# A diffusion backbone's first projection: products from raw streams, feature tile by feature tile, and modulation products 512 columns wide

## Chip, core and metric

One NeuronCore of a Trainium2 chip runs the whole program. The metric is the device time of one execution in microseconds (us), lower is better.

## What is computed

Two layers over 512 latent tokens and 256 context tokens of 1024 features. Layer 0 mixes tokens by latent attention (MLA), layer 1 by a gated linear recurrence (HGRN2); each is followed by a SwiGLU FFN. Every sub-layer takes a normalized input that is scaled and shifted by values ("modulation") made from a vector c, one set for latent and one for context tokens. The part around the change, cut from the reference:

```python
def rms_norm(x, w):
    y = x * lax.rsqrt(jnp.mean(x * x, axis=-1, keepdims=True) + EPS)
    return y * w

mod_l = jnp.split(jax.nn.silu(c) @ ada_w[i] + ada_b[i], 6, axis=-1)        # shift, scale, gate, shift, scale, gate
mod_c = jnp.split(jax.nn.silu(c_ctx) @ ada_w[i] + ada_b[i], 6, axis=-1)
a_l = rms_norm(x, norm1_w[i]) * (1 + mod_l[1]) + mod_l[0]
a_c = rms_norm(h_ctx, norm1_w[i]) * (1 + mod_c[1]) + mod_c[0]
...
# MLA, for latent and context tokens alike
cq, ckv, kr = jnp.split(a @ w_in, [384, 384 + 256], axis=-1)               # w_in: 1024 x 704
q = split_heads(rms_norm(cq, q_norm_w) @ w_uq, 8)
kv = split_heads(rms_norm(ckv, kv_norm_w) @ w_ukv, 8)
k_rope = rms_norm(kr, kr_w)
```

## The kernel before

Features lie on the 128 partitions: a stream is 8 feature tiles (`KD`) by 768 tokens (`NT`), in 6 token tiles, 0 to 3 latent and 4, 5 context. Products run in fp32r with operands split in a high and a low half: high by high, high by low and low by high, three matmuls for one product (`mm3m`, L101 to L110; `mm3`, L92 to L99).

**Modulation** (`ada`, L150 to L168). 96 units of 128 columns, 48 for each layer; layer 0's units 0 to 7 are the first sub-layer's shift, 8 to 15 its scale. A call makes n units (always 4). Each unit loads one tile of 512 KB, [128, 8 feature tiles x 128 columns], into one of four slots of the ring `wf`, and runs 8 f32 matmuls with a stationary operand of 32 columns, feature tile k into partitions 32 (k mod 4) on, that is, into one of four column groups of the array; the profile shows each as two passes (L158). ScalarE copies the rows out of PSUM, TensorE transposes them, VectorE adds the four groups and the bias.

**The input projection** (`mla_in`, L324 to L424). SP's queue issues all loads in the order of the program: first x (16 loads), then modulation units 0 to 3 and 8 to 11, WIN for features 0 to 3, units 4 to 7 and 12 to 15, WIN 4 to 7, the tables BC and ROPE. ScalarE squares x and VectorE adds up (L187 to L194); a transpose, a reduction, a power on GpSimd and an f32 matmul against ones spread each token's factor over all partitions (`norm_rb`, L197 to L217). Then, in two halves of four feature tiles, `norm` (L219 to L232) writes the normalized, scaled and shifted activations in two halves, a_hi and a_lo, and the WIN weights are split, high by ScalarE (L359), low by GpSimd (L360). `proj` (L383 to L396) multiplies: per token tile 8 feature tiles, 384 and 320 columns, three matmuls each; tiles 0 and 1 together, then 2, 3, 4, 5. For each token tile follow squares on ScalarE (L407), the three root factors (`rsqrt`), the normalized c (L412, L413), the rotary part on GpSimd, six transposes into the one PSUM buffer `tp2` (L419), and the copies into cn_hi, kr_hh (L420, L421) and cn_lo, kr_lo (L422, L423).

**Attention** (`mla_attend`) starts from cn_hi and cn_lo. The WUP weights are loaded into `wf`, cast by ScalarE (L83) and split by GpSimd (L84). For every head and group of three token tiles come products, squares (L470), factors, rotary steps on GpSimd, transposes (L489), then scores (L514 to L518). In heads 1 to 7 `ada` calls for later sub-layers stand behind the head at a lowered priority (`ADA_HEAD`, `ada_m`).

**Order.** The Tile framework plans the order on each engine from its own costs: of what is ready by them it takes what stands first in the program, moved by the priorities in `PRIO`. PSUM has eight banks: `sc` and `tp2` of two banks each, `ov`, two `L`, one `M`.

## Time and profile before

| | us |
|---|---|
| median of 3 runs | 1847.92 |
| lowest and highest run | 1844.15, 1857.01 |
| the profiled execution | 1853.65 |
| its span, first to last instruction | 1851.9 |

A profile shows one execution of the program. "Busy" is the time in which an engine works on an instruction; a matmul's end is modelled, so starts tell more than ends. A row of the timeline gives start, duration, engine, line, operation, out<-in by the program's names and, in brackets, the engine's idle time before it and what ended that. PE is TensorE, DVE VectorE, ACT ScalarE, POOL GpSimd, SP the queue that issues DMAs.

### The profile page before, as it was taken

Reading aid. Unit: us, or ns where it says so; the run is one execution under the profiler, and the core shown is the slowest. Engines: PE = TensorE matmul, PEld = TensorE weight load, DVE = VectorE, ACT = ScalarE, POOL = GpSimd, SP = SyncE. Lnnn points to the kernel's source line nnn. Section 1 sums busy time; section 2 is a strip of 40 time slices with the busy share of each in tenths; the row PEclk is TensorE's granted clock in tenths of the full one; section 3 lists DMA queues with packets and bytes.
Section 4 is the critical chain, followed back from the end, with each engine's and each line's share of the span. In section 5 each row is a group of like instructions: output and inputs, shape, how many; then the busy total and the mean of one; then the engine's idle time right before and its main releaser. Section 6 shows DMA issues by size and latency. Waiting matters only on the chain. (4 is left out here: it accounts for less than half of the span.)

```text
span 1851.9 us, 33106 instructions
## 1 busy us (share of the span) xinstructions
PE 1755.5 (95%) x13708; PEld 1591.8 (86%) x13708; DVE 1016.3 (55%) x1646; ACT 762.6 (41%) x1467; POOL 760.6 (41%) x528
## 2 busy tenths in 40 slices
PE   4889999999899999999999999999998889999999
PEld 3878989788799999988887888888896779999888
DVE  5567887741754445432203666575745278888400
ACT  4355565532554344432213332423333255555411
POOL 2333342216566666643344554554643440000442
PEclk9999999999999999999999999999999989999999
DMA  7412032523222322254224121111115233333331
GB/s 268 137 39 73 25 116 98 170 74 122 103 86 97 104 96 103 81 168 136 86 71 148 60 69 47 61 55 58 58 35 191 94 137 103 103 115 103 108 118 49
DMA packets 55015, 183.61 MB, mean 99 GB/s; under 512 B 6224, under 2 KB 8528, under 8 KB 54864
## 3 DMA queue, kind: packets, MB, share of 16 engines
q1 hardware_dynamic: 53424, 173.62, 28.5%
q10 hardware_dynamic: 1440, 7.86, 1.2%
q8 instruction: 108, 1.77, 0.4%
q14 instruction: 43, 0.35, 0.1%
HBM read 171.50 MB, written 9.96 MB: 98 GB/s over the span
## 5 line engine op out<-in xcount | busy, mean ns | idle before, releaser
L84 POOL TENSOR_TENSOR wl<-wf,wh 128x1024 fp32r<-128x1024 f32 (+2 forms) x130 | 287.0, 2214 | 438.9 <-ACT wh L83 436.5
L83 ACT CAST wh<-wf 128x1024 fp32r<-128x1024 f32 (+2 forms) x130 | 122.9, 947 | 226.2 <-PE L L98 102.5
L97 PE MATMUL q<-op,sh 128*128 128x384 f32 (+1 forms) x640 | 197.3, 310 | 1.0 <-ACT sh L622 1.0
L98 PE MATMUL q<-op,sh 128*128 128x384 f32 (+1 forms) x640 | 197.6, 310 | 0.0
L99 PE MATMUL q<-op,sl 128*128 128x384 f32 (+1 forms) x640 | 194.9, 310 | 0.0
L97 PEld LDWEIGHTS q<-op,sh 128*128 128x128 f32 x640 | 120.3, 188 | 1.5 <-ACT sh L622 1.5
L98 PEld LDWEIGHTS q<-op,sh 128*128 128x128 f32 x640 | 120.3, 188 | 0.0
L99 PEld LDWEIGHTS q<-op,sl 128*128 128x128 f32 x640 | 119.5, 188 | 0.0
L623 POOL TENSOR_TENSOR sl<-wf,sh 128x1024 fp32r<-128x1024 f32 (+1 forms) x40 | 88.7, 2218 | 56.4 <-ACT sh L622 56.4
L98 PE MATMUL L<-op,sh 128*128 128x256 f32 (+1 forms) x360 | 110.4, 307 | 0.0
L99 PE MATMUL L<-op,sl 128*128 128x256 f32 (+1 forms) x360 | 110.3, 306 | 0.0
L97 PE MATMUL L<-op,sh 128*128 128x256 f32 (+1 forms) x360 | 110.3, 306 | 0.0
L1060 DVE TENSOR_TENSOR X<-X,T 128x512 f32<-128x512 f32 x96 | 78.1, 855 | 47.0 <-PE lv L985 45.9
L557 DVE SCALAR_TENSOR_TENSOR xl<-L,mod,xl 128x512 f32<-128x512 f32 x24 | 17.9, 750 | 153.8 <-PE L L99 149.8
L622 ACT CAST sh<-wf 128x1024 fp32r<-128x1024 f32 x80 | 66.7, 834 | 70.2 <-PE L L98 32.7
L98 PE MATMUL L<-f_lo,wh 128*128 128x512 f32 (+1 forms) x240 | 89.1, 371 | 0.0
L97 PE MATMUL L<-f_hi,wh 128*128 128x512 f32 (+1 forms) x240 | 89.0, 371 | 0.0
L99 PE MATMUL L<-f_hi,wl 128*128 128x512 f32 (+1 forms) x240 | 88.5, 369 | 0.0
L158 PE MATMUL L<-adaw,s 128*32 128x128 f32 x1216 | 57.1, 297 | 29.5 <-DMA adaw<-in_ADA 29.3
L975 POOL TENSOR_SCALAR km<-X 128x512 f32<-128x512 f32 x40 | 29.4, 737 | 125.5 <-DVE X L1060 76.4
L622 ACT CAST sh<-sb 128x1024 fp32r<-128x1024 f32 x40 | 42.0, 1050 | 88.5 <-PE q L98 46.6
L158 PEld LDWEIGHTS L<-adaw,s 128*32 128x32 f32 x1216 | 34.8, 116 | 46.1 <-DMA adaw<-in_ADA 17.2
(466 smaller groups left out, 5585.3 us busy)
## 6 DMA issues: line engine op xcount, KB each, us to landing
wf<-in_W SPq DMA_DIRECT2D x104, 512.0 KB, 3.5
adaw<-in_ADA SPq DMA_DIRECT2D x96, 512.0 KB, 4.4
wf<-in_HW SPq DMA_DIRECT2D x32, 512.0 KB, 3.5
wf<-in_W SPq DMA_DIRECT2D x24, 384.0 KB, 3.2
gd<-s SPq DMA_DIRECT2D x10, 768.0 KB, 3.5
g<-gd ACTq DMA_DIRECT2D x10, 768.0 KB, 4.7
wf<-in_W SPq DMA_DIRECT2D x16, 320.0 KB, 3.0
wf<-in_MWO SPq DMA_DIRECT2D x8, 512.0 KB, 4.1
```

Of the source, the lines that this page charges most:

```text
L83: nc.scalar.copy(hi[:, :n], w[:, :n])
L84: nc.gpsimd.tensor_sub(lo[:, :n], w[:, :n], hi[:, :n].bitcast(F32))
L97: nc.tensor.matmul(out, lhsT=lh, rhs=rh, start=(new and i == 0), stop=False, skip_group_check=more)
L98: nc.tensor.matmul(out, lhsT=lh, rhs=rl, start=False, stop=False, skip_group_check=more)
L99: nc.tensor.matmul(out, lhsT=ll, rhs=rh, start=False, stop=(i == n - 1), skip_group_check=more)
L158: nc.tensor.matmul(rows_ps[32 * j:32 * j + 32, i * P:(i + 1) * P], lhsT=self.s32[:, k, :], rhs=w[:, k * P:(k + 1) * P], start=(k < 4), sto ...
L557: nc.vector.scalar_tensor_tensor(xk, po, gate[:, s:s + 1], xk, op0=ALU.mult, op1=ALU.add)
L622: nc.scalar.copy(hi[:, :n], s)
L623: (nc.vector if j in on_dve else nc.gpsimd).tensor_sub(lo[:, :n], s, hi[:, :n].bitcast(F32))
L975: nc.gpsimd.tensor_scalar(km.rearrange("p (m b r) -> p m b r", b=2, r=L), mix, 1.0, 0.0, op0=ALU.mult, op1=ALU.add)
L1060: nc.vector.tensor_tensor(v, v, t, op=ALU.mult)
```

## The change

- **Raw products.** `mla_in` splits x itself into x_hi and x_lo and scales the WIN weights instead: `scaled(k, s)` makes high and low halves of WIN's feature tile k times norm weight times (1 + scale), for latent (s = 0) or context tokens (s = 1), the high half on ScalarE, the low on VectorE. The factor of each token and the shift come in afterwards, in `norms`: product times the token's factor, plus the row shift @ WIN.
- **Loop over feature tiles.** Loads of x, scale units, WIN and shift units are interleaved by pairs of features. Each feature tile is multiplied at once for tiles 0 to 3 (512 and 192 columns) and for 512 columns of tile 4; the rest of tile 4 and tile 5 follow behind the loop (`left`), with the weights scaled anew. All raw weights are kept, in the memory where cn_hi and cn_lo come to lie.
- **Shift rows** (`shift_rows`), inside the loop between feature tiles 6 and 7: f32 products of the shifts with the raw weights, through column groups and a summing matrix, all through the one bank `M`.
- **Norms by pairs** of token tiles, out of an SBUF copy; **turn** does the transposes and copies for all six tiles behind the loop and `left`. The first WUP weights are fetched ahead of `turn`.
- **Wide modulation.** `ada` loads the same bytes cut the other way: a load holds RING / (128 n) feature tiles by all n units' columns. With n = 4 that is two feature tiles by 512 columns, with n = 2 (the new calls in `mla_in`) four by 256; a call of four units has 8 matmuls of 512 columns instead of 32 of 128.

```diff
+NIN = QR + KVR + DR
+WUP_CUT = ((0, 768), (768, 1664))
...
-PRIO = {"hg_head": 1000, "ada_m": -500, "ada_n": -300}
+PRIO = {"shw": 600, "hg_head": 1000, "ada_m": -500, "ada_n": -300}
...
     def ada(self, l, u0, n, pool, bank):
         nc = self.nc
         rows_ps = bank()
-        for i in range(n):
+        g, c0 = divmod(u0, 4)
+        src = self.a["ADA"][l, g].rearrange("p (k c) -> p k c", k=KD)[:, :, c0 * P:(c0 + n) * P]
+        kn = RING // (n * P)
+        for k0 in range(0, KD, kn):
             w = self.ring.tile([P, RING], F32, tag="wf", name="adaw", bufs=4)
-            nc.sync.dma_start(out=w[:, :D], in_=self.a["ADA"][l, u0 + i])
-            for k in range(KD):
+            nc.sync.dma_start(out=w.rearrange("p (k c) -> p k c", k=kn), in_=src[:, k0:k0 + kn])
+            for k in range(k0, k0 + kn):
                 j = k % 4
-                nc.tensor.matmul(rows_ps[32 * j:32 * j + 32, i * P:(i + 1) * P], lhsT=self.s32[:, k, :],
-                                 rhs=w[:, k * P:(k + 1) * P], start=(k < 4), stop=(k >= 4))
+                nc.tensor.matmul(rows_ps[32 * j:32 * j + 32, :n * P], lhsT=self.s32[:, k, :],
+                                 rhs=w[:, (k - k0) * n * P:(k - k0 + 1) * n * P], start=(k < 4), stop=(k >= 4))
...
-    def mla_in(self, es, mla, a_hi, a_lo):
+    def mla_in(self, es, mla, x_hi, x_lo):
...
-        w_hi = st.tile([P, KD, 704], F32R, name="w_hi")
-        w_lo = st.tile([P, KD, 704], F32R, name="w_lo")
+        wp = self.pool(es, "wp", side="right")
+        shw = wp.tile([P, 2, NIN], F32, name="shw")
+        rms = wp.tile([P, 2, TT], F32, name="rms")
...
-        with ExitStack() as es1:
-            ap = self.pool(es1, "adap")
-            x = [ap.tile([P, KD, c1 - c0], F32, name=f"x0{s}") for s, c0, c1 in SEGS]
-            for k in range(KD):
...
-                    self.sq_add(ap, acc, x[s][:, k, :], s, k, c0, c1, nc.vector, 2)
-            rb = ps.tile([P, NT], F32, tag="tp2", name="rb")
...
-                    self.ada(0, k0, 4, ap, self.M)
-                    self.ada(0, KD + k0, 4, ap, lambda: ps.tile([P, 512], F32, tag="ov", name="ov"))
-                self.norm_scale(0, 0, ks)
-                self.norm(0, 0, x, rbs, SEGS, ap, a_hi, a_lo, ks)
-                for k in ks:
-                    w = self.ring.tile([P, RING], F32, tag="wf", name="wf", bufs=4)
-                    last = nc.sync.dma_start(out=w[:, :704], in_=a["WIN"][:, k, :])
-                    nc.scalar.copy(w_hi[:, k, :], w[:, :704])
-                    nc.gpsimd.tensor_sub(w_lo[:, k, :], w[:, :704], w_hi[:, k, :].bitcast(F32))
-
-        with self.tc.issue_after(last.ins):
-            nc.sync.dma_start(out=bc, in_=a["BC"].partition_broadcast(P))
-            nc.sync.dma_start(out=rt, in_=a["ROPE"])
-        self.cn = cn = self.pool(mla, "cn")
...
+        wide, even = ((0, 512), (512, NIN)), ((0, QR), (QR, NIN))
+        def scaled(k, s):
+            sc = self.nsc[(0, 0)][:, k, s:s + 1]
+            hi, lo = (wp.tile([P, NIN], F32R, tag=n, name=f"w_{n}", bufs=3) for n in ("hi", "lo"))
+            nc.scalar.activation(hi, raw[k], AF.Identity, scale=sc)
+            nc.vector.scalar_tensor_tensor(lo, raw[k], sc, hi.bitcast(F32), op0=ALU.mult, op1=ALU.subtract)
+            return hi, lo
+        def products(outs, k, w):
+            hi, lo = w
+            for o, t, (c0, c1), new, end in outs:
+                c = slice(t * P, (t + 1) * P)
+                mm = nc.tensor.matmul
+                mm(o, lhsT=x_hi[:, k, c], rhs=hi[:, c0:c1], start=(k == 0 and new), stop=False)
+                mm(o, lhsT=x_hi[:, k, c], rhs=lo[:, c0:c1], start=False, stop=False)
+                mm(o, lhsT=x_lo[:, k, c], rhs=hi[:, c0:c1], start=False, stop=(k == KD - 1 and end))
+        def norms(t0, sums):
+            p2 = wp.tile([P, 2, NIN], F32, tag="pre", name="pre", bufs=2)
+            for o, t, (c0, c1), _, _ in sums:
+                if t0 <= t < t0 + 2:
+                    nc.vector.scalar_tensor_tensor(p2[:, t - t0, c0:c1], o, rms[:, 1, t:t + 1], shw[:, t0 // 4, c0:c1], op0=ALU.mult, op1=ALU.add)
...
+            r = tmp.tile([P, 2, 3], F32, tag="r", name="r")
+            self.rsqrt(r.rearrange("p a b -> p (a b)"), ss.rearrange("p a b -> p (a b)"), tmp, "in")
+            c = tmp.tile([P, 2, 6, P], F32, tag="c", name="c", bufs=2)
+            m = tmp.tile([P, 2, DR], F32, tag="m", name="m")
+            nc.vector.tensor_tensor(m, p2[:, :, 640:NIN], r[:, :, 2:3].broadcast_to([P, 2, DR]), op=ALU.mult)
+            self.rope(c[:, :, 5, :], m, ktab[:, t0:t0 + 2], tmp)
+            for i in range(2):
+                cf = c[:, i].rearrange("p a b -> p (a b)")
+                for j, w0 in ((0, BC_Q), (1, BC_KV)):
+                    c0, c1 = cuts[j]
+                    nc.vector.scalar_tensor_tensor(cf[:, c0:c1], p2[:, i, c0:c1], r[:, i, j:j + 1], bc[:, w0:w0 + c1 - c0], op0=ALU.mult, op1=ALU.mult)
+            return c
+        def turn(t0, c):
+            for i in range(2):
+                ts = slice((t0 + i) * P, (t0 + i + 1) * P)
+                tp = ps.tile([P, 6, P], F32, tag="tp2", name="tp")
+                for j in range(6):
+                    nc.tensor.transpose(tp[:, j, :], c[:, i, j, :], self.ident)
+                nc.scalar.copy(cn_hi[:, :, ts], tp[:, 0:5, :])
+                nc.scalar.copy(kr_hh[:, ts], tp[:, 5, :])
+                nc.vector.tensor_sub(cn_lo[:, :, ts], tp[:, 0:5, :], cn_hi[:, :, ts].bitcast(F32))
+                nc.vector.tensor_sub(kr_lo[:, ts], tp[:, 5, :], kr_hh[:, ts].bitcast(F32))
...
+        self.cn = cn = self.pool(mla, "cn")
+        raw = [cn.tile([P, 4, NIN], F32, tag=t, name="raw") for t in ("cn_hi", "cn_lo")]
+        raw = [raw[k // 4][:, k % 4] for k in range(KD)]
...
+        with ExitStack() as es1:
+            ap = self.pool(es1, "adap")
+            acc = ap.tile([P, NT], F32, name="acc")
...
+            big = [ps.tile([P, 1024], F32, tag=tag, name="pp") for tag in ("sc", "tp2")]
+            rest = [self.L() for _ in range(2)]
+            ov = ps.tile([P, 512], F32, tag="ov", name="ov")
+            lat = [(big[t // 2][:, 512 * (t % 2):512 * (t % 2) + 512], t, wide[0], True, True) for t in range(4)]
+            lat += [(rest[t // 2][:, 192 * (t % 2):192 * (t % 2) + 192], t, wide[1], t % 2 == 0, t % 2 == 1) for t in range(4)]
+            lat = [lat[i] for t in range(4) for i in (t, 4 + t)]
+            for k0 in range(0, KD, 2):
+                ks = range(k0, k0 + 2)
+                for k in ks:
+                    xk = self.ring.tile([P, NT], F32, tag=("wh", "wl")[k % 2], name="xk", bufs=3)
+                    nc.sync.dma_start(out=xk, in_=a["XT"][:, k, :])
+                    nc.scalar.copy(x_hi[:, k, :], xk)
+                    nc.vector.tensor_sub(x_lo[:, k, :], xk, x_hi[:, k, :].bitcast(F32))
+                    if k == 0:
+                        nc.scalar.activation(acc, xk, AF.Square)
+                        continue
+                    sq = ap.tile([P, NT], F32, tag="sq", name="sq", bufs=2)
+                    nc.scalar.activation(sq, xk, AF.Square)
+                    if k == KD - 1:
+                        nc.vector.scalar_tensor_tensor(acc, acc, EPS * KD, sq, op0=ALU.add, op1=ALU.add)
+                    else:
+                        nc.vector.tensor_add(acc, acc, sq)
+                self.ada(0, KD + k0, 2, ap, self.M)
+                self.norm_scale(0, 0, ks)
+                for k in ks:
+                    if k < KD - 1:
+                        nc.sync.dma_start(out=raw[k], in_=a["WIN"][:, k, :])
+                    if k == KD - 2:
+                        for c0, c1 in ((0, 4), (4, TT)):
+                            tp = self.M()
+                            for t in range(c0, c1):
+                                nc.tensor.transpose(tp[:, (t - c0) * P:(t - c0 + 1) * P], acc[:, t * P:(t + 1) * P], self.ident)
+                            nc.vector.tensor_reduce(rms[:, 0, c0:c1], tp[:, :(c1 - c0) * P].rearrange("p (t f) -> p t f", f=P), axis=AX.X, op=ALU.add)
+                        nc.gpsimd.tensor_tensor(rms[:, 1, :], rms[:, 0, :], self.half.broadcast_to([P, TT]), op=ALU.pow)
+                        nc.vector.tensor_scalar(rms[:, 1, :], rms[:, 1, :], math.sqrt(D), None, op0=ALU.mult)
+                    products(lat, k, scaled(k, 0))
+                    products([(ov, 4, wide[0], True, True)], k, scaled(k, 1))
+                    if k == KD - 2:
+                        nc.sync.dma_start(out=raw[k + 1], in_=a["WIN"][:, k + 1, :])
+                        self.ada(0, k0, 2, ap, self.M)
+                        self.shift_rows(ap, raw, sel, shw, wide)
+                if k0 < KD - 2:
+                    self.ada(0, k0, 2, ap, self.M)
+            nc.sync.dma_start(out=bc, in_=a["BC"].partition_broadcast(P))
+            nc.sync.dma_start(out=rt, in_=a["ROPE"])
+            table(ktab, BC_KR, 1.0)
+            cs = [norms(t0, lat) for t0 in (0, 2)]
+            big = ps.tile([P, 1024], F32, tag="sc", name="pp")
+            rest = [self.L() for _ in range(2)]
+            left = [(rest[0][:, :192], 4, wide[1], True, True), (big[:, 0:QR], 5, even[0], True, True), (rest[1][:, :320], 5, even[1], True, True)]
+            for k in range(KD):
+                products(left, k, scaled(k, 1))
+            for c0, c1 in WUP_CUT:
+                self.fetch("WUP", (0,), c0, c1)
+            table(qtab, BC_QR, SCALE)
+            nc.vector.scalar_tensor_tensor(wqk, bc[:, BC_QN:BC_QN + DN], SCALE, bc[:, BC_KN:BC_KN + DN], op0=ALU.mult, op1=ALU.mult)
+            cn_hi, cn_lo = (self.cn.tile([P, 5, NT], F32R, tag=t, name=t) for t in ("cn_hi", "cn_lo"))
+            self.lat = (cn_hi, cn_lo, kr_hh, kr_lo, wqk, qtab)
+            for t0 in (0, 2, 4):
+                turn(t0, cs[t0 // 2] if t0 < 4 else norms(4, left + [(ov, 4, wide[0], True, True)]))
         self.dump("cn_hi", cn_hi.bitcast(F32))
         self.dump("kr_hh", kr_hh.bitcast(F32))
+    def shift_rows(self, ap, raw, sel, shw, cut):
+        nc = self.nc
+        shb = ap.tile([P, KD, 2, 16], F32, name="shb")
+        nc.vector.tensor_copy(shb, self.mod[0][:, 0:KD, :].unsqueeze(3).broadcast_to([P, KD, 2, 16]))
+        rows = ap.tile([P, NIN], F32, tag="sq", name="shrow", bufs=2)
+        for c0, c1 in cut:
+            po = self.M()[:, :c1 - c0]
+            for k in range(KD):
+                j = k % 4
+                nc.tensor.matmul(po[32 * j:32 * j + 32, :], lhsT=shb[:, k].rearrange("p s c -> p (s c)"), rhs=raw[k][:, c0:c1],
+                                 start=(k < 4), stop=(k >= 4))
+            nc.scalar.copy(rows[:, c0:c1], po)
+        for s in range(2):
+            for c0, c1 in cut:
+                po = self.M()[:, :c1 - c0]
+                nc.tensor.matmul(po, lhsT=sel[:, s, :], rhs=rows[:, c0:c1], start=True, stop=True)
+                nc.scalar.copy(shw[:, s, c0:c1], po)
 
...
-                wq0, wq1 = (self.weight("WUP", (h // 2,), c0, c1) for c0, c1 in ((0, 768), (768, 1664)))
+                wq0, wq1 = (self.weight("WUP", (h // 2,), c0, c1) for c0, c1 in WUP_CUT)
...
-    d["ADA"] = np.stack([cols(f["ada_w"][l], P) for l in range(2)])
+    d["ADA"] = np.stack([cols(f["ada_w"][l], 4 * P) for l in range(2)])
```

## Rows read from the trace of the kernel before

**Rows 1.** The page: TensorE's busy tenths in 40 slices of 46 us.
```profile
PE   4889999999899999999999999999998889999999
```

**Rows 2.** Stretches: length, each engine's busy us (count), granted TensorE clock, DMA share, GB/s.
```profile
0.00:20.00 20.00, 2.85 (x36) 1.97 (x36) 8.78 (x25) 10.38 (x20) 0.69 (x6) 1.00 0.81 273
...
36.00:40.00 4.00, 4.00 (x30) 3.58 (x28) 3.96 (x6) 1.50 (x3) 1.06 (x1) 0.63 0.69 241
...
120.00:145.00 25.00, 17.35 (x143) 13.86 (x143) 19.52 (x47) 11.40 (x33) 16.65 (x21) 0.86 0.38 119
...
200.00:260.00 60.00, 59.07 (x486) 54.39 (x487) 52.23 (x125) 35.86 (x97) 21.98 (x29) 1.00 0.11 41
```

**Rows 3.** TensorE's timeline, 17 to 35 us: start, us, what [idle before <-releaser].
```profile
17.03 2.28 PE L158 MATMUL L<-adaw,s 128*32 128x128 f32 x32 [17.03 <-DMA adaw<-in_ADA]
...
23.98 1.13 PE L215 MATMUL rb<-dg,ones 128*128 128x512 f32 x2
...
25.61 0.70 PE L215 MATMUL rb<-dg,ones 128*128 128x256 f32 x2
...
34.22 0.69 PE L108 MATMUL L<-w_hi,a_hi 128*128 128x384 f32 x1 [5.09 <-ACT a_hi L230]
```

**Rows 4.** Timeline of TensorE and ScalarE, 99 to 136 us: from projection to first scores.
```profile
99.01 0.82 PE L419 MATMUL tp<-ident,c 128*128 128x128 f32 x6
102.16 0.85 PE L419 MATMUL tp<-ident,c 128*128 128x128 f32 x6 [2.33 <-DVE w L245]
...
113.73 1.02 ACT L470 ACTIVATE sq<-arena 128x960 f32<-128x960 f32 x1
...
119.71 0.38 PE L489 MATMUL M<-ident,arena 128*128 128x128 f32 x2
...
121.16 1.02 ACT L470 ACTIVATE sq<-arena 128x960 f32<-128x960 f32 x1
...
132.21 0.69 PE L489 MATMUL M<-ident,arena 128*128 128x128 f32 x2
...
135.52 0.49 PE L514 MATMUL sc<-qk_hi 128*128 128x512 f32 x1 [0.21 <-ACT qk_hi L490]
```

**Rows 5.** TensorE's timeline: matmuls of 512 and 256 columns in a row.
```profile
149.34 0.39 PE L518 MATMUL sc<-kr_lo,qk_hi 128*128 128x512 f32 x1
149.57 0.28 PE L514 MATMUL sc<-qk_hi 128*128 128x256 f32 x1
149.68 0.28 PE L515 MATMUL sc<-qk_lo,qk_hi 128*128 128x256 f32 x1
```

**Rows 6.** TensorE's timeline: modulation passes in runs of 16, 2 and 32.
```profile
40.72 0.64 PE L158 MATMUL M<-adaw,s 128*32 128x128 f32 x16
...
177.12 0.41 PE L158 MATMUL L<-adaw,s 128*32 128x128 f32 x2
...
177.93 1.08 PE L158 MATMUL L<-adaw,s 128*32 128x128 f32 x32
```

**Rows 7.** VectorE's groups by shape, 0 to 115 us: count | busy us, mean ns.
```profile
L228 DVE SCALAR_TENSOR_TENSOR nx<-x,nsc,rb 128x512 f32<-128x512 f32 x8 | 5.9, 743 | 0.1
...
L228 DVE SCALAR_TENSOR_TENSOR nx<-x,nsc,rb 128x256 f32<-128x256 f32 x8 | 3.8, 474 | 0.0
...
L413 DVE SCALAR_TENSOR_TENSOR c<-pp,r,bc 128x256 f32<-128x256 f32 x4 | 1.9, 476 | 0.0
L412 DVE SCALAR_TENSOR_TENSOR c<-pp,r,bc 128x384 f32<-128x384 f32 x3 | 1.9, 618 | 0.2
```

**Rows 8.** Timeline of VectorE and GpSimd where both work, 29 to 67 us.
```profile
29.31 4.93 POOL L360 TENSOR_TENSOR w_lo<-wf,w_hi 128x704 fp32r<-128x704 f32 x3 [5.27 <-ACT w_hi L359]
...
32.66 2.19 DVE L228 SCALAR_TENSOR_TENSOR nx<-x,nsc,rb 128x512 f32<-128x512 f32 x4
...
61.09 5.79 POOL L84 TENSOR_TENSOR wl<-wf,wh 128x768 fp32r<-128x768 f32 x3 [2.50 <-ACT wh L83]
...
61.11 6.05 DVE L231 SCALAR_TENSOR_TENSOR a_lo<-nx,mod,a_hi 128x256 fp32r<-128x256 f32 x3
```

**Rows 9.** TensorE's groups, 130 to 420 us: modulation passes, count | busy us, mean ns.
```profile
L158 PE MATMUL L<-adaw,s 128*32 128x128 f32 x640 | 31.6, 288 | 1.4 <-DMA adaw<-in_ADA 1.4
```

More of the change, by code (lines that the diff above doesn't have):

```diff
@@ L362, in mla_in @@
-        with self.tc.issue_after(last.ins):
-            nc.sync.dma_start(out=bc, in_=a["BC"].partition_broadcast(P))
-            nc.sync.dma_start(out=rt, in_=a["ROPE"])
-        self.cn = cn = self.pool(mla, "cn")
-        cn_hi, cn_lo = (cn.tile([P, 5, NT], F32R, tag=t, name=t) for t in ("cn_hi", "cn_lo"))
-        kr_hh = cn.tile([P, NT], F32R, name="kr_hh")
-        kr_lo = cn.tile([P, NT], F32R, name="kr_lo")
-        wqk = cn.tile([P, DN], F32, name="wqk")
-        qtab = cn.tile([P, TT, 2, DR], F32, name="qtab")
@@ L371, in mla_in @@
-        self.lat = (cn_hi, cn_lo, kr_hh, kr_lo, wqk, qtab)
-        nc.vector.scalar_tensor_tensor(wqk, bc[:, BC_QN:BC_QN + DN], SCALE, bc[:, BC_KN:BC_KN + DN], op0=ALU.mult, op1=ALU.mult)
-        for tab, w0, f in ((qtab, BC_QR, SCALE), (ktab, BC_KR, 1.0)):
-            w = bc[:, w0:w0 + DR]
-            nc.vector.scalar_tensor_tensor(tab[:, :, 0, :], rt[:, :, 0, :], f, w.unsqueeze(1).broadcast_to([P, TT, DR]),
+        wide, even = ((0, 512), (512, NIN)), ((0, QR), (QR, NIN))
[5 more added lines that the diff above has]
+            return hi, lo
@@ new lines, in products @@
+        def products(outs, k, w):
[11 more added lines that the diff above has]
+                    nc.vector.scalar_tensor_tensor(p2[:, t - t0, c0:c1], o, rms[:, 1, t:t + 1], shw[:, t0 // 4, c0:c1], op0=ALU.mult, op1=ALU.add)
+            ss = tmp.tile([P, 2, 3], F32, tag="ss", name="ss")
+            junk = tmp.tile([P, QR], F32, tag="junk", name="junk", bufs=1)
+            cuts = ((0, QR), (QR, 640), (640, NIN))
+            for i in range(2):
+                for j, (c0, c1) in enumerate(cuts):
+                    nc.scalar.activation(junk[:, :c1 - c0], p2[:, i, c0:c1], AF.Square, scale=1.0 / math.sqrt(c1 - c0), accum_out=ss[:, i, j:j + 1])
+            r = tmp.tile([P, 2, 3], F32, tag="r", name="r")
[10 more added lines that the diff above has]
+            return c
@@ new lines, in turn @@
+        def turn(t0, c):
+            for i in range(2):
+                ts = slice((t0 + i) * P, (t0 + i + 1) * P)
[6 more added lines that the diff above has]
+                nc.vector.tensor_sub(kr_lo[:, ts], tp[:, 5, :], kr_hh[:, ts].bitcast(F32))
@@ L376, in mla_in, with table @@
+        def table(tab, w0, f):
+            wr = bc[:, w0:w0 + DR]
+            nc.vector.scalar_tensor_tensor(tab[:, :, 0, :], rt[:, :, 0, :], f, wr.unsqueeze(1).broadcast_to([P, TT, DR]),
                                            op0=ALU.mult, op1=ALU.mult)
@@ L380, in mla_in @@
                                                ws.unsqueeze(1).broadcast_to([P, TT, 16]), op0=ALU.mult, op1=ALU.mult)
-        def proj(ts):
-            pab = []
-            for t in ts:
-                if t in (1, 3, 4):
-                    pp = ps.tile([P, 1024], F32, tag="tp2" if t == 3 else "sc", name="pp")
-                    pab.append((pp[:, :QR], pp[:, 512:832]))
-                else:
-                    second = ps.tile([P, 512], F32, tag="ov", name="pp") if t == 2 else self.L()
-                    pab.append(((self.M() if t == 2 else self.L())[:, :QR], second[:, :320]))
-            self.mm3m([(pab[i][j], [((a_hi[:, k, t * P:(t + 1) * P], a_lo[:, k, t * P:(t + 1) * P]),
-                                     (w_hi[:, k, c0:c1], w_lo[:, k, c0:c1])) for k in range(KD)])
-                       for i, t in enumerate(ts) for j, (c0, c1) in enumerate(((0, QR), (QR, 704)))])
-            return pab
@@ L424, in mla_in @@
         self.dump("cn_hi", cn_hi.bitcast(F32))
         self.dump("kr_hh", kr_hh.bitcast(F32))
+    def shift_rows(self, ap, raw, sel, shw, cut):
[10 more added lines that the diff above has]
+            nc.scalar.copy(rows[:, c0:c1], po)
+        for s in range(2):
+            for c0, c1 in cut:
+                po = self.M()[:, :c1 - c0]
+                nc.tensor.matmul(po, lhsT=sel[:, s, :], rhs=rows[:, c0:c1], start=True, stop=True)
+                nc.scalar.copy(shw[:, s, c0:c1], po)
```

46 lines of the change are left out of this document (9 added, 37 removed).

## Prediction, made before the changed kernel was seen

> **What bounds the kernel now.** I read the page's slices first: TensorE is at 9 tenths nearly everywhere, so the time is its work plus its holes, and the holes lie at the very start, with a few near the three quarters [rows 1]. Then the table of stretches: TensorE is busy 2.85 of the first 20 us and again only 17.4 of the 25 from 120 to 145, but 59.1 of 60 from 200 to 260, at the full clock, and so it goes on [rows 2]. What ends earlier before about 145 us is therefore kept, and what is added to TensorE's work behind it is paid.
>
> The timeline says why the start is empty. The first product of the input projection runs at 34.22 us. Before it TensorE waited 17.03 us for the first tile of modulation weights (the queue loads all of x ahead of it) and 5.09 us for the first normalized activation [rows 3]: norm, scale and shift stand ahead of every product. The projection takes until 99 us. Then comes a chain of small steps. Token tiles are turned one after the other (99.01, 102.16 for two in a row); the sums of squares of the first three tiles run at 113.73, of the last three at 121.16; their transposes begin at 119.71 and 132.21, the first scores at 135.52 [rows 4].
>
> **The loop.** The change projects raw x with weights scaled per feature, so that a product needs one x tile, one scale and one WIN tile, and no norm.
>
> Loads: the same bytes (3.1 MB of x, 8.4 of modulation weights, 2.9 of WIN), all on SP's queue as before, and nothing that another stage waits for is moved past them. At the 273 GB/s of the first 20 us [rows 2] they last 53 us; TensorE's work below is longer. The modulation rows become pieces of 1 KB here. No row shows their rate; if it were a sixth lower, the stream would last 63 us, still under the work, and a higher one would change nothing.
>
> First product: by 17.03 us all of x and one modulation tile are down, 3.7 MB. Two x tiles, two modulation loads and a WIN tile are 2.2 MB: 10 us in proportion. Then the modulation step and the scaled weight: 1.2 us of passes, 0.4 copy, 0.4 transposes, 0.6 small VectorE steps and 0.8 for the scaled weight, estimates by the like steps in the rows below. So 14 us, against 34.2.
>
> TensorE per feature tile: matmuls of 512 columns start 0.23 us apart, of 256 columns 0.11 to 0.12 [rows 5]; six transposes of 128 columns in 0.82 us are 0.11 each [rows 4]. So 192 columns cost 0.115. Four token tiles at 512 and 192, one at 512, three matmuls each: 12 x 0.345 + 3 x 0.23 = 4.83 us, over 8 tiles 38.6. (Cutting at 512 instead of 384 costs some 2 us of it.) Modulation: 14 loads behind the first two at 0.64 us, as one unit standing alone now [rows 6], since a load of 256 columns again fills the array's four column groups: 9.0, with transposes 10.5. Shift rows: f32 products of 512 and 256 columns take 1.13 and 0.70 us for two passes [rows 3]; with two of 512, two of 192 and two over column groups, 5.5. Clock: the first products before, after the pause, ran at 0.63 of it from 36 to 40 us [rows 2]; the loop begins behind a pause too: 2.5. For the chain modulation, scale, weight at each of the three later pairs of features I take a wait of 1 us: 3 (0 if the next pair's modulation always finds a place between products, 4 each if never). Sum: 14 + 38.6 + 10.5 + 5.5 + 2.5 + 3 = 74 us.
>
> **Behind the loop** TensorE has tile 5 and the rest of tile 4: 8 x 3 x (0.115 + 0.175 + 0.147), by the line between 256 and 512 columns, 10.5 us. VectorE does more in that stretch. It moves four tiles out of PSUM (4 x 0.743 and 4 x 0.38), does two norms (each twice 0.618 + 0.476, and some 1 us of small steps: 3.2) and five of eight low halves of the scaled weights (0.95 each by the 512- and 256-column rows; three lie ready): 4.5 + 6.4 + 4.7 = 15.6 [rows 7]. I take 16. The new cn_hi and cn_lo lie where the raw weights lay, so no tile is turned before the last scaled weight is made. In that time GpSimd splits the first WUP weights. Three such splits stretched three VectorE steps of 256 columns from 3 x 0.474 to 6.05 us; beside another split, four steps that read PSUM took their usual 2.19 [rows 7, 8]. I take 2 us: turning begins at 92.
>
> The Trainium skill bears on this: the page "SBUF — State Buffer", section "SBUF: two separate sides", says that a VectorE step with two SBUF inputs and a GpSimd step that reads SBUF shut each other out for a whole instruction. The trace agrees [rows 8]. It speaks against the change: the norms' wide steps read PSUM and one SBUF table before and read two SBUF tiles now, and the low halves of the weights move from GpSimd to VectorE, with two SBUF inputs. By the rule alone all three splits, 5.8 us, would be lost here, and the sum below would be 4 us higher.
>
> Six turns at 3.15 us, with one transposing buffer: 111. The last tile's products and copies: 3, so the last squares run at 114 instead of 121.16. From there to the transposes it was 11 us, against 6 for the first three tiles [rows 4], whose steps lay across it; that changes, and of the 5 I take 3. The start gains 7 + 3 = 10 us. Ends: without waits and lock, and with TensorE as the bound behind the loop, 18; with waits of 4 us, the full lock and none of the 3, a loss of 6.
>
> **Wide modulation products.** Outside this stage 80 units remain, in 20 calls. A unit is 16 passes of 128 columns over four column groups. Two passes, one group, last 0.41 us, sixteen 0.64, thirty-two 1.08 [rows 6]: groups run side by side, a round of four takes 0.11, and some 0.2 is tail and change of shape. So columns set the time, not the count of instructions. The wide form has as many columns, but a load holds two of the eight feature tiles, hence two groups: two rounds of 0.44 and 0.2, 1.07 us alone against 0.64, and as much as now if the next load stands right behind it (1.07 for both). From 130 to 420 us 640 passes, 40 units, are busy for 31.6 us, 0.79 each [rows 9]: the planner cuts them up as fillers. TensorE has no time to give there, so I count half of these 40 loads as alone: 20 x 0.43, 8 us. The other 40 lie around changes of stage where TensorE waits anyway, as from 120 to 145 [rows 2]: 0, or 9 more if that cover is gone. Ends: whole calls give 11 us back (ten calls at 4 x 0.79 against 1.95); every load alone costs 34.
>
> **Sum.** -10 + 8 = -2 us on the profiled execution's 1853.65 us (span 1851.9, and 1.75 around it). That execution lies 5.7 us over the median of the three runs, so 1847.9 - 2: **1846 us**. The order of all later instructions is planned anew from the planner's own costs; I give that no sign.
>
> **Rivals.**
> (a) *The start is filled.* Modulation always finds a place, nothing locks, and wide calls stay whole, because eight instructions can't be cut as fine as thirty-two: -18 - 6 = -24, 1824 us. For it: loads and products are independent, and TensorE waits for the first scale alone. Against it: VectorE is the bound behind the loop by my count.
> (b) *Wide loads stand alone.* The place is the modulation line in the attention heads and at the changes of stage, the price 0.43 us for every load that meets only two column groups. With all 80 alone: -10 + 34 = +24, 1872 us. It decides over 1% from (18.5 + 10) / 0.43 = 66 loads alone. For it: 0.79 us a unit shows the cutting. Against it: half of the units lie where TensorE has time.
> (c) *The turn is late.* The alias keeps the tiles waiting, and waits and locks take their high ends: +6 + 8 = +14, 1862 us.
> (d) *The loads set the pace.* Then the loop ends near 63 us plus the last tile's products, no later than 74, and nothing changes.
>
> **How the numbers follow.** Forecast 0.42, (a) 0.31, (b) 0.18, (c) 0.09. The forecast's own range is 1832 to 1860. Within 1% is 1829.4 to 1866.4, about what a measurement of this kernel can tell from no change. Faster by over 1%: 0.27 of (a) and 0.03 of the forecast, 0.30. Slower: 0.15 of (b) and 0.03 of (c), 0.18. Same: 0.52. The range for 8 in 10 takes in (a)'s 1824 with 6 us for its own bounds, 1818, and stops just short of (b)'s 1872, at 1869.
>
> **What would show it.** Right: the first projection product near 14 us, tile 3's last product near 74, VectorE nearly full from there to 92, first scores near 125, and the modulation line busy for more than 31.6 us in the attention heads. Wrong: TensorE idle for over 4 us at each pair of features; the modulation line busy for less than 31.6 us (then columns are not its price); a first score after 135.

## The result and the profile after

The changed kernel takes 1867.22 us (median of 4 runs, 1864.73 to 1869.38) against 1846.6 us: ratio 1.0116, 95% interval 1.0084 to 1.0149. Run once more, beside the last experiments: 1867.45 us, ratio 1.0095 (1.0076 to 1.0115). It is slower by about 1%. Its profiled execution took 1866.33 us. That of before lay 7 us over its median, so the two profiles show only 12.7 of the 20 us; I compare them by stretches and lean on the timed runs for sums.

The page's slices of the changed kernel, then its table of stretches (columns as in [rows 2]):

```profile
PE   6889999989899999989999999999998889999999
```

```profile
0.00:20.00 20.00, 9.40 (x52) 4.73 (x53) 11.49 (x28) 12.48 (x18) 0.69 (x6) 1.00 0.90 309
20.00:40.00 20.00, 15.78 (x88) 11.70 (x87) 14.10 (x29) 9.27 (x13) 0.00 (x0) 0.83 0.95 332
40.00:60.00 20.00, 18.21 (x123) 13.11 (x122) 5.67 (x12) 5.20 (x8) 0.00 (x0) 1.00 0.42 132
...
200.00:260.00 60.00, 56.16 (x407) 51.14 (x406) 49.22 (x113) 34.37 (x92) 18.07 (x24) 1.00 0.12 41
```

The start did fill (9.40 us busy of the first 20, 2.85 before), but in the heads TensorE now misses 3.8 us of 60 where it missed 0.9 [rows 2].

**The start.** Timelines of TensorE, VectorE and ScalarE in the changed kernel:

```profile
14.44 0.80 PE L357 MATMUL pp<-w_hi,a_hi 128*128 128x512 f32 x1
...
71.56 2.96 DVE L348 SCALAR_TENSOR_TENSOR w_lo<-raw,nsc,w_hi 128x704 fp32r<-128x704 f32 x2 [0.69 <-ACT w_hi L347]
...
77.23 0.40 PE L359 MATMUL ov<-w_hi,a_lo 128*128 128x512 f32 x1
77.87 1.82 DVE L348 SCALAR_TENSOR_TENSOR w_lo<-raw,nsc,w_hi 128x704 fp32r<-128x704 f32 x2 [0.31 <-ACT w_hi L347]
...
80.32 0.86 PE L503 MATMUL M<-raw,shb 128*32 128x192 f32 x16 [0.69 <-ACT shrow L505]
81.62 1.12 PE L509 MATMUL M<-shrow,sel 128*128 128x512 f32 x2 [0.44 <-ACT shrow L505]
...
83.40 2.73 DVE L366 SCALAR_TENSOR_TENSOR pre<-pp,rms,shw 128x512 f32<-128x512 f32 x4 [3.72 <-ACT shw L510]
...
94.70 0.70 ACT L392 CAST cn_hi<-tp 128x640 fp32r<-128x640 f32 x1 [0.53 <-DVE w_lo L348]
...
99.99 0.95 DVE L348 SCALAR_TENSOR_TENSOR w_lo<-raw,nsc,w_hi 128x704 fp32r<-128x704 f32 x1 [1.17 <-ACT w_hi L347]
100.97 0.82 DVE L394 TENSOR_TENSOR cn_lo<-tp,cn_hi 128x640 fp32r<-128x640 f32 x1
...
104.12 0.69 ACT L392 CAST cn_hi<-tp 128x640 fp32r<-128x640 f32 x1 [4.16 <-PE tp L391]
...
139.22 0.48 PE L599 MATMUL sc<-qk_hi 128*128 128x512 f32 x1
```

The first product runs at 14.44 us (34.22 before, [rows 3]) and the loop's last at 77.23. Only then do the shift rows come, step by step through the one bank M, each waiting for ScalarE's copy of the one before. VectorE stands idle for 3.72 us until the first of them is copied: the norms begin at 83.40. The last scaled weight is made at 99.99, and right behind it comes the first cn_lo, which lies in the raw weights' memory. The second tile's copy waits for that until 104. First scores: 139.22, against 135.52 [rows 4].

**The heads**, from the first softmax maximum to the end of the last head: first the stretch, the modulation passes in it and TensorE's wait for the softmax (us in total, times, longest) in the kernel before; then the same of the changed kernel, with the passes from 130 to 420 us as a last row beside [rows 9].

```profile
145.48:418.50 273.02, 263.00 (x2193) 233.16 (x2192) 201.75 (x455) 149.09 (x365) 75.64 (x85) 0.99 0.27 92
```

```profile
L158 PE MATMUL L<-adaw,s 128*32 128x128 f32 x576 | 27.7, 279 | 1.4 <-DMA adaw<-in_ADA 1.4
```

```profile
PE sc L514 <- ACT p L524: 1.7, 3, 1.1
```

```profile
148.14:419.48 271.34, 253.93 (x1738) 214.72 (x1737) 197.52 (x452) 148.72 (x361) 78.58 (x85) 0.99 0.27 90
```

```profile
PE sc L599 <- ACT p L609: 6.1, 8, 1.5
```

```profile
L163 PE MATMUL L<-adaw,s 128*32 128x512 f32 x144 | 24.8, 632 | 0.0
...
L163 PE MATMUL L<-adaw,s 128*32 128x512 f32 x160 | 28.0, 665 | 0.0
```

The wide passes are cheaper, 24.8 us against 27.7 (all 40 units from 130 to 420 us: 28.0 against 31.6 [rows 9]), but TensorE is idle for 17.4 us (length less busy) instead of 10.0, above all before scores, which wait for the last softmax to leave their bank.

**The norm of layer 1**, 997 to 1030 us and 1000 to 1038: the stretch and TensorE's timeline in the kernel before, then in the changed one.

```profile
997.30:1029.73 32.43, 28.60 (x260) 21.84 (x259) 23.77 (x46) 16.29 (x28) 8.24 (x7) 1.00 0.46 166
```

```profile
1001.02 0.64 PE L158 MATMUL L<-adaw,s 128*32 128x128 f32 x14
1001.59 0.66 PE L205 MATMUL q<-ident,acc 128*128 128x128 f32 x4
...
1006.11 0.43 PE L158 MATMUL L<-adaw,s 128*32 128x128 f32 x8 [2.29 <-DMA adaw<-in_ADA]
1006.47 1.12 PE L215 MATMUL q<-dg,ones 128*128 128x512 f32 x2
```

```profile
1000.50:1038.03 37.53, 32.97 (x164) 19.89 (x163) 24.74 (x47) 16.65 (x28) 7.68 (x7) 0.95 0.41 143
```

```profile
1004.22 1.91 PE L163 MATMUL L<-adaw,s 128*32 128x512 f32 x12
1006.06 0.88 PE L210 MATMUL q<-ident,acc 128*128 128x128 f32 x6
...
1009.35 1.05 PE L163 MATMUL L<-adaw,s 128*32 128x512 f32 x4 [2.41 <-DMA adaw<-in_ADA]
1011.09 0.97 PE L169 MATMUL M<-ident,rows 128*128 128x128 f32 x4 [0.69 <-ACT rows L166]
1011.85 1.92 PE L220 MATMUL q<-dg,ones 128*128 128x512 f32 x2
```

In these timelines TensorE's instructions run one behind the other in the planned order. Before, the chain of the norm (transposes of the sums, then the product that spreads the factors) stood behind 0.57 us and 0.36 us of modulation; now it stands behind 1.84 us and, with a wait and the transposes of the rows, 2.50 us, and that product takes 1.92 us instead of 1.12. The stretch is 5.1 us longer. Against a kernel with narrow products there and the same granted clock of 0.95 (33.57 us, "wide in the heads" below) about 4 us are left.

### The profile page after: what moved, and what is told of

Read it like the earlier page. It is cut to its first block, busy times and chain, and to the rows that moved or that the text cites. A ratio compares the mean times of both kernels' runs of the same rounds, so it can differ in the third digit from the quotient of the medians.

```text
span 1864.5 us, 30972 instructions
## 1 busy us (share of the span) xinstructions
PE 1765.7 (95%) x12656; PEld 1556.3 (83%) x12656; DVE 1024.8 (55%) x1650; ACT 775.5 (42%) x1471; POOL 745.9 (40%) x507
## 5 line engine op out<-in xcount | busy, mean ns | idle before, releaser
L99 PE MATMUL L<-gs,wh 128*128 128x512 f32 x180 | 70.3, 391 | 2.7 <-ACT gs L713 2.7
L100 PE MATMUL L<-gs,wh 128*128 128x512 f32 x180 | 70.4, 391 | 2.1 <-DVE gs L714 2.1
```

Of the source, the lines that this page charges most:

```text
L99: nc.tensor.matmul(out, lhsT=lh, rhs=rh, start=(new and i == 0), stop=False, skip_group_check=more)
L100: nc.tensor.matmul(out, lhsT=lh, rhs=rl, start=False, stop=False, skip_group_check=more)
```

## Experiments

All at a glance: ratio to the kernel before on the same chip, the first norm copy out of PSUM, the first scores, length and TensorE's idle time of the heads, length of the layer 1 norm (us, from the profiles). The profile of before is of an execution 7 us over its median, so its lengths are long; idle times compare better.

| kernel | ratio (95%) | norm copy | scores | heads, idle | norm 1 |
|---|---|---|---|---|---|
| before | 1 | | 135.5 | 273.0, 10.0 | 32.4 |
| changed | 1.0116 (1.0084 to 1.0149) | 83.4 | 139.2 | 271.3, 17.4 | 37.5 |
| wide alone | 1.0073 (1.0047 to 1.0099) | | 132.9 | 274.5, 18.3 | 37.0 |
| loop alone | 1.0004 (0.9986 to 1.0022) | 80.7 | 138.7 | 265.1, 9.6 | 33.0 |
| no shift rows | 1.0075 (1.0049 to 1.0101) | 73.5 | 129.4 | 280.8, 20.3 | 36.5 |
| wide loads, narrow matmuls | 1.0256 (1.0229 to 1.0283) | 82.2 | 142.2 | 288.2, 8.4 | 38.0 |
| 256 columns | 1.0108 (1.0080 to 1.0135) | 82.0 | 137.7 | 276.0, 16.8 | 37.1 |
| shift rows before | 1.0033 (1.0017 to 1.0050) | 89.0 | 143.3 | 266.1, 9.9 | 35.0 |
| wide in the heads | 1.0026 (1.0008 to 1.0045) | 82.6 | 138.4 | 274.3, 18.5 | 33.6 |
| own bank | 0.9989 (0.9974 to 1.0004) | 75.4 | 135.0 | 267.9, 10.3 | 33.9 |
| changed, again | 1.0095 (1.0076 to 1.0115) | 82.6 | 138.4 | 273.8, 18.2 | 37.5 |

**The two halves of the change.** First the kernel before with the new `ada` and packing only, then the changed kernel with the old ones (there the lines are those of the change's diff, the other way round).

```diff
-    d["ADA"] = np.stack([cols(f["ada_w"][l], P) for l in range(2)])
+    d["ADA"] = np.stack([cols(f["ada_w"][l], 4 * P) for l in range(2)])
...
-            for k in range(KD):
+            for k in range(k0, k0 + kn):
```

> The kernel before with the wide modulation products alone (input projection as before). Theory W, the wide products cost the time at the changes of stage behind the heads, where the changed kernel lost 11 of its 12.4 us against the profiled execution of before: about +15 us against before, near 1862. Rival S, the loop's late start costs it: about -3 us, near 1844, the 3 us that the modulation line lost in the heads (30.3 to 27.4 us).

> The changed kernel with the modulation products as before, 128 columns a matmul, the loop over feature tiles kept. Theory W: within 5 us of before, 1845 to 1852. Rival S: about as the changed kernel, 1867. Rival O, neither part costs it by itself and the newly planned order of the later stages does: both kernels of this pair lie between, and the matmuls of 256 columns in the last FFN start 120.0 ns apart in one or both, as in the changed kernel, instead of 118.7.

Medians 1859.53 and 1849.15 us, before 1849.39. The loop alone changes nothing, as theory W had it; the wide products alone cost 0.7% (13 us by the ratio, 10 between the medians), somewhat under W's 15. But W put the loss behind the heads, and the table has idle time in the heads as well in every kernel with wide products there, 17 to 20 us against 10. Of rival O, the last FFN's slower matmuls do appear in the loop alone, at no loss in time.

**Without shift rows.**

```diff
-                        self.shift_rows(ap, raw, sel, shw, wide)
+                        nc.vector.memset(shw, 0.0)
```

> The changed kernel without the shift rows: their table is filled with zeros, so the shift's part of the first projection is left out; the shift's modulation products still run. If the norms wait for the shift rows (their first copy from PSUM comes at 83.40 us, 6.2 us behind tile 3's last product), that copy moves to about 78 us, the first copy into cn_hi from 94.7 to about 89, the first softmax maximum by as much, and the time falls by 3 to 6 us. Rival: VectorE and the memory shared with the raw weights hold the turn; then the first cn_hi copy stays within 2 us of 94.7 and the time within 3 us of 1867.

The first norm copy in VectorE's timeline, the stretch of the heads, and the wait for the softmax in it:

```profile
73.47 1.39 DVE L366 SCALAR_TENSOR_TENSOR pre<-pp,rms,shw 128x512 f32<-128x512 f32 x2
```

```profile
138.45:419.21 280.76, 260.42 (x1764) 221.08 (x1763) 202.12 (x454) 149.35 (x365) 77.39 (x85) 0.98 0.27 88
```

```profile
PE sc L599 <- ACT p L609: 10.1, 9, 4.2
```

The norms start 9.9 us earlier, more than expected, and the first scores 9.8 (129.40): the chain of the shift rows stood wholly on the path. The time falls by only 4.4 us (1862.84; 4 to 8 by the ratios, whose intervals overlap), for the heads grow from 271.3 to 280.8 us, with 10.1 us of waiting for the softmax. In the two profiles nothing of the earlier start is left at the end of the heads, 419.21 us against 419.48. About half of it went in one place, with a single wait before scores:

```profile
178.71 0.79 PE L599 MATMUL sc<-qk_hi 128*128 128x512 f32 x1 [4.22 <-ACT p L609]
```

Behind that wait TensorE's granted clock was 0.81 from 178.7 to 190.5 us; in the changed kernel it was 1.00 over the same work. A start that comes earlier can be lost in the next stage; "The start" below has kernels that keep it.

**Which property of the wide products?** Two forms between: the wide load with 128-column matmuls, and calls in two halves of 256 columns by four features.

```diff
-                nc.tensor.matmul(rows_ps[32 * j:32 * j + 32, :n * P], lhsT=self.s32[:, k, :],
-                                 rhs=w[:, (k - k0) * n * P:(k - k0 + 1) * n * P], start=(k < 4), stop=(k >= 4))
+                for i in range(n):
+                    nc.tensor.matmul(rows_ps[32 * j:32 * j + 32, i * P:(i + 1) * P], lhsT=self.s32[:, k, :],
+                                     rhs=w[:, ((k - k0) * n + i) * P:((k - k0) * n + i + 1) * P], start=(k < 4 and i == 0),
+                                     stop=(k >= 4 and i == n - 1), skip_group_check=True)
```

> The changed kernel with its wide loads (two feature tiles by 512 columns), but matmuls of 128 columns again, 32 for a call of four. Theory F, the loss in the heads comes from calls that the planner can cut only in lumps of 1 us and more, so that they no longer fill TensorE's short waits for the softmax: the modulation runs in the heads rise from 20 towards 43, TensorE's idle time from the first softmax to the last head falls from 16 us to about 10, and the time to 1850 to 1856. Rival L, the loads do it, since a load holds only two of the eight features and so two column groups: idle time stays at 16 or the passes cost more than 31.6 us, and the time stays at 1862 or over.

```diff
-        for k0 in range(0, KD, kn):
+        for h in range(0, n, 2):
+            for k0 in range(0, KD, 4):
...
+                    nc.tensor.matmul(rows_ps[32 * j:32 * j + 32, h * P:(h + 2) * P], lhsT=self.s32[:, k, :],
+                                     rhs=w[:, (k - k0) * 2 * P:(k - k0 + 1) * 2 * P], start=(k < 4), stop=(k >= 4))
```

> The changed kernel with every call of four units made as two halves of 256 columns: a load holds four feature tiles by 256 columns and fills all four column groups, a call has 16 matmuls. Theory F (lumps): about half of the loss comes back, 1854 to 1860, idle time in the heads 12 to 14 us. Rival L (two column groups a load): the whole loss comes back, 1849 to 1853.

The modulation passes in the heads and TensorE's wait for the softmax there, with narrow matmuls on wide loads, then with 256 columns:

```profile
L164 PE MATMUL L<-adaw,s 128*32 128x128 f32 x576 | 50.0, 277 | 0.0
```

```profile
PE sc L601 <- ACT p L611: 2.2, 2, 1.1
```

```profile
L161 PE MATMUL L<-adaw,s 128*32 128x256 f32 x288 | 23.4, 386 | 0.3 <-DMA adaw<-in_ADA 0.3
```

```profile
PE sc L597 <- ACT p L607: 5.2, 6, 2.4
```

F misses both times and L the second, and each has half of the rows. With 128-column passes the idle time is down to 8.4 us and the softmax waits to 2.2, as F says; but the same 576 passes now take 50.0 us instead of 27.7, as L feared, since a load's passes come eight in a row for one column group, and the time goes up to 1896.72. (Part of the fall in idle time may be those longer passes themselves.) With 256 columns and all four column groups the passes cost least, 23.4 us, yet the idle time stays at 16.8 and the time at 1870.22: L's price isn't what the changed kernel pays. What remains with F is how finely a call is cut, as a theory. The timeline of the loop alone shows what the narrow passes do, that of the changed kernel what is there instead:

```profile
265.60 0.63 PE L160 MATMUL L<-adaw,s 128*32 128x128 f32 x12
266.16 0.39 PE L596 MATMUL sc<-qk_hi 128*128 128x256 f32 x1
...
353.40 0.41 PE L160 MATMUL L<-adaw,s 128*32 128x128 f32 x4
353.75 0.50 PE L596 MATMUL sc<-qk_hi 128*128 128x512 f32 x1
```

```profile
262.08 1.91 PE L163 MATMUL L<-adaw,s 128*32 128x512 f32 x12
...
266.87 0.39 PE L599 MATMUL sc<-qk_hi 128*128 128x256 f32 x1 [0.48 <-ACT p L609]
...
271.30 0.50 PE L599 MATMUL sc<-qk_hi 128*128 128x512 f32 x1 [1.47 <-ACT p L609]
```

Four to twelve narrow passes stand just where the scores would wait. Counted over 130 to 420 us, the loop alone has 40 such runs, 10 of them right before scores; the changed kernel has 20, 3 of them before scores. The kernel with 256 columns has 27, 6 of them before scores, and as much idle time as the changed one, so the count alone doesn't explain it. That the idle time rises because the fine passes no longer fill the waits is argued, not shown, and that the planner's choice, and not the length of a pass by itself, makes the difference wasn't tried.

**Where: heads or later calls.** Narrow and wide weights are both packed; input projection and heads use the wide ones.

```diff
...
-                    self.ada(u // 48, u % 48, 4, tmp, self.L)
+                    self.ada_w(u // 48, u % 48, 4, tmp, self.L)
...
```

> The changed kernel with wide products in the input projection and the attention heads alone; the ten later calls, at the norms, in the FFNs and the recurrence, have 128 columns. The two profiles put 6 us of the wide products' loss in the heads and 4.5 at the norm of layer 1: then the stretch of that norm goes back from 37.5 to 33 us, the heads keep 16 us of idle time, and the time is 1853 to 1860. Rival: all of it lies at the later changes of stage, 1847 to 1851. Rival: all in the heads, 1864 or more.

The norm of layer 1 is back at 33.6 us, the heads keep 18.5 us of idle time, the time is 1855.52: inside the expected range. Against the loop alone the heads (with the projection's own calls) cost 0.2%, which the two intervals can't tell from nothing. The profiles show it more plainly: from the first scores to the end of the heads the three kernels with the loop and the wide 512-column products there (this one and the changed one twice) take 280.3 to 283.5 us, the three with narrow ones (loop alone, shift rows before, own bank) 275.1 to 276.9. The ten later calls cost the other 0.7 to 0.9%, clear of noise.

Of those 13 to 17 us the profiles place 4 at the norm of layer 1. Another 2 us lie in the last FFN, but they don't go with the width: the loop alone has them, the wide products alone have not (see the last section). A third place shows when the same weight splits of GpSimd are set beside each other in all profiles, here the 94th to the 103rd, in the kernel before and in the changed one (stretch, length, TensorE's busy us, its granted clock, DMA):

```profile
1358.98:1473.88 114.90, 102.59 (x1036) 0.96 0.38 124
```

```profile
1363.40:1481.67 118.27, 104.77 (x845) 0.94 0.36 121
```

The five kernels whose later calls are wider than 128 columns take 117.9 to 121.5 us here, at a clock of 0.92 to 0.94; the five with narrow loads and products there take 111.0 to 114.9, at 0.95 to 0.97. Some of it is no net loss: ahead of it, from the 82nd split on, the wide five take 129.0 to 130.4 us at 0.99 to 1.00 and four of the narrow five 133.6 at 0.96. What sets the clock and the waits there was not tried, and the rest of the 13 to 17 us is not placed.

**The start.** On the loop alone, the shift rows put before the products of features 6 and 7, with the shift units and WIN loaded one pair earlier; then also with a bank of their own, for which tile 4 leaves the loop.

```diff
+                    if k == KD - 2:
+                        nc.sync.dma_start(out=raw[k + 1], in_=a["WIN"][:, k + 1, :])
+                        self.shift_rows(ap, raw, sel, shw, wide)
...
```

> The loop with modulation products of 128 columns, and the shift rows made before the products of features 6 and 7 instead of between and behind them (the last shift units and WIN tiles are loaded one pair earlier). If the chain of the shift rows is what holds the start: first norm copy from PSUM at 73 to 77 us instead of 80.7, first scores at 131 to 135 instead of 138.7, time 1842 to 1846, faster than both kernels. Rival: the chain through the one bank M stays as late, or the token factors now wait behind it: first scores at 137 or later and the time within 3 us of 1849.

The end of the shift rows, the transposes of the token sums behind them, and the first norm copy:

```profile
84.04 0.59 PE L506 MATMUL M<-shrow,sel 128*128 128x192 f32 x2 [0.68 <-ACT shw L507]
85.05 0.66 PE L458 MATMUL M<-ident,acc 128*128 128x128 f32 x4 [0.41 <-ACT shw L507]
...
89.04 0.75 DVE L363 SCALAR_TENSOR_TENSOR pre<-pp,rms,shw 128x512 f32<-128x512 f32 x1
```

The rival's second half holds: the token factors need bank M too and now wait behind the shift rows, so the norms start at 89.04, and the kernel is slower than the loop alone (1855.54), by more than the rival's 3 us. The bank is the queue.

```diff
-                    products([(ov, 4, wide[0], True, True)], k, scaled(k, 1))
...
-            left = [(rest[0][:, :192], 4, wide[1], True, True), (big[:, 0:QR], 5, even[0], True, True), (rest[1][:, :320], 5, even[1], True, True)]
+            left = [(ov, 4, wide[0], True, True), (rest[0][:, :192], 4, wide[1], True, True), (big[:, 0:QR], 5, even[0], True, True), (rest[1][:, :320], 5, even[1], True, True)]
...
+        bank = lambda: self.ps_mla.tile([P, 512], F32, tag="ov", name="sv")
-            po = self.M()[:, :c1 - c0]
+            po = bank()[:, :c1 - c0]
```

> The loop with modulation products of 128 columns, four token tiles at once instead of five: the bank of tile 4 goes to the shift rows, which then run beside the modulation and the token factors instead of behind them in bank M; the shift units of features 6 and 7 are loaded a pair earlier; tile 4 is multiplied behind the loop with tile 5. Theory: the start was held by the chain through the one bank M. Then the first norm copy from PSUM comes at 70 to 75 us (80.7 in the loop alone, 89.0 with the shift rows ahead of the token factors), first scores at 126 to 132 (before: 135.5), and the time is 1840 to 1846, the fastest yet. Rival: what the start gains is lost again in the heads, as 9.8 us without shift rows brought only 4.4: then first scores are early, and the time is within 3 us of before.

The first norm copy in VectorE's timeline and the first scores in TensorE's:

```profile
75.42 1.41 DVE L363 SCALAR_TENSOR_TENSOR pre<-pp,rms,shw 128x512 f32<-128x512 f32 x2 [1.03 <-PE pp L356]
...
134.98 0.47 PE L597 MATMUL sc<-qk_hi 128*128 128x512 f32 x1
```

The norms now wait for the products themselves, at 75.42 us, a little over the expected 75. The scores, at 134.98, miss the expected 126 to 132. In its timeline the last scaled weight, for tiles 4 and 5, is made at 94.23 and the first cn_lo follows at 95.69: it seems the memory shared with the raw weights that holds the turn now. At 1846.55 us it is the fastest kernel of the study, 1% under the changed one, but not to be told from before. Raw weights in memory of their own, which would show it, were not tried.

Here an earlier start is mostly kept. The heads of the loop alone, of the kernel with the shift rows before and of this one, columns as above:

```profile
148.80:413.93 265.13, 255.50 (x2166) 226.87 (x2164) 200.01 (x454) 147.98 (x361) 74.67 (x83) 1.00 0.28 91
```

```profile
152.26:418.36 266.10, 256.25 (x2170) 227.53 (x2169) 201.49 (x452) 148.71 (x361) 76.92 (x85) 1.00 0.28 92
```

```profile
143.99:411.84 267.85, 257.57 (x2183) 229.02 (x2182) 200.91 (x453) 149.48 (x362) 77.77 (x86) 1.00 0.28 93
```

With the first scores at 138.7, 143.3 and 135.0 us the heads end at 413.93, 418.36 and 411.84, in the same order and four fifths as far apart, and the times are 1849.15, 1855.54 and 1846.55.

**The changed kernel again**, with no edit.

> The changed kernel as it is, once more, on the chip of the run beside it. If its loss is its own and not that of one chip: 1864 to 1870, 15 to 20 us over before. And whether the 161.2 us that its last FFN took from the fourth to the twentieth weight split, against 159.4 in before, is the kernel's or the execution's: 159.4 in this profile would make it the execution's.

1867.45 us: the loss is the kernel's. The last FFN takes 161.2 us again, so the 1.8 us in it may be the kernel's too; two equal values don't settle that.

## Why the prediction was wrong

I forecast no change, with 0.18 for slower by over 1%, and the kernel is slower by about 1%. The sum was -10 us for the start, +8 for the loads in the heads and 0 for the other 40 loads. The runs gave 0 for the loop alone (ratio 1.0004), about 4 for the wide products in the heads (0.2% over the loop alone, not clear of noise) and 13 to 17 for the ten later calls. So two steps failed: the start's gain, and above all the term for the other 40 loads, which I put at nothing because TensorE waits around the changes of stage anyway. That the time lies inside the range (1818 to 1869), near rival (b)'s 1872, is luck: (b) made every load dear by standing alone, and the passes became cheaper.

- **First product at 14 us**: 14.44. Right.
- **The loop's sum, 74 us.** It counted the shift rows as 5.5 us of TensorE's work inside the loop. This is the first step of the start that failed: they are a chain of six steps through one bank behind it, and the norms began at 83.40. Without them they began at 73.47. The waits at the pairs were undersized too: TensorE was idle 6.0 us from 20 to 60 us alone, against 3 for the whole.
- **VectorE's 16 us behind the loop, and the turn behind the last scaled weight.** The count was right, the place 9 us late: 83.40 to 100.9 is 17.5.
- **The last squares to the scores.** I took 3 of 5 us as gained. In the changed kernel the last squares before the scores' transposes ran at 125.87 and the scores at 139.22: 13.4 us, against 14.4 before [rows 4], so 1 was gained. Without shift rows it was 16.9, in the loop alone 16.7.
- **"What ends earlier before about 145 us is kept."** Not always: of 9.8 us without shift rows nothing was left at the end of the heads, but among the three kernels with the loop and narrow products 8.3 us between the first scores were still 6.5 at the end of the heads.
- **Columns set the price of a modulation pass.** Right: one wide load alone lasts 1.05 us (estimated 1.07), two in a row 1.06, a whole call 1.92 (1.95). But I took half of the loads as alone; 9 of 40 were, and the line fell to 28.0 us from 31.6 [rows 9], which by my own test should have refuted the price.
- **Wide products in the heads, +8 us.** The sign was right, the reason wrong. I priced the passes by their own length, which fell, and left out what they may fill: the idle time of the heads rose by 7 to 9 us.
- **The other 40 loads, 0.** This is the largest miss, 13 to 17 us. A wait of TensorE covers a longer load only where the chain that it waits for doesn't stand behind that load. At the norm of layer 1 it does: it stood in TensorE's queue behind the loads, and the stretch grew by 5.1 us, 4 of them at a like clock. Where most of the rest arises stays open.

Both parts together cost 13 us in the kernel before and 17 to 21 beside the loop, by the ratios. Two slips in the sums, 20 x 0.43 taken as 8 and ten calls at 1.21 as 11, shift nothing.

In the changed kernel the memory shared between raw weights and cn_hi, cn_lo seems to hold the turn as rival (c) said, since the first cn_lo follows the last scaled weight at once; no run tested it, and in the loop alone that weight was made at 91.87 and the first cn_hi came only at 96.22. The lock between VectorE and GpSimd (the Trainium skill, "SBUF — State Buffer", "SBUF: two separate sides") shows again: two low halves at 71.56 us, beside GpSimd splits that ran from 69.01 to 72.91, took 2.96 us, two at 77.87, with none beside them, 1.82. It seems to have cost nothing in the time, since VectorE then waited 3.72 us for the shift rows.

## What to carry to other kernels

Price work by what stands behind it in its engine's queue, and not by its own length alone: merging 32 small instructions to 8 made the passes cheaper and the kernel slower. That an engine waits in a stage is no cover for longer work there if the chain that it waits for must pass through the same queue. Ask of every moved step which single buffer it shares, and what queues there behind it. And follow an earlier start to the end of the next stage before counting it: here three kernels kept most of the difference and one lost all of its gain.

## What the runs showed of the hardware

- The same 576 passes, 277 to 279 ns each, took 27.7 us when consecutive ones went to four column groups and 50.0 us when eight in a row went to one: the order in the queue, and not the count, made the difference.
- In the last FFN, matmuls of 256 columns started 118.7 ns apart in the profile of before and 120.0 ns apart in both of the changed kernel, from an unchanged part of the program: 2 us. Between the same two weight splits six profiles of the study show 159.4 us and five 161.2 (the changed kernel twice, loop alone, wide loads with narrow matmuls, own bank), always the same 1343 matmuls; what sets it is open.
- At the norm of layer 1 the product that spreads the factors took 1.92 us where the granted clock was 0.50 (1011.85 to 1013.80 us in the changed kernel), the lower of the two levels, and 1.12 where it was 1.00. Over the stretch of 37.5 us the mean of 0.95 makes 3.8 us at the lower level; TensorE had stood idle for 2.41 and 0.69 us just ahead of it.
